# Triangular inverse by columns instead of rows, key decay as a per-token scalar, and smaller first query scalings in a hybrid decoder layer

## The chip, the core and the metric

The program runs on one core of a Trainium2 chip. The metric is the device time of one execution in microseconds (us). Before the change it is 2710.9 us, the median of three runs (2706.43 to 2711.62).

A core has a matrix engine (PE; its weight loads are listed apart as PEld), a vector engine (DVE), a scalar engine with activation functions (ACT), a general engine (POOL), and a queue that only issues DMAs (SP). Each works through its own list of instructions in order, and waits at an instruction until what it needs has been signalled.

## The reference

One layer, 2048 tokens of width 1024, all in fp32. One input projection feeds four heads of a gated delta rule and four heads of HGRN2; their outputs go through one output projection, a squared-ReLU MLP with 4096 hidden units, and a gated embedding. The change lies in the two token mixers:

```python
def gated_delta_rule_chunked(q, k, v, g, beta):
    ...
    gc = jnp.cumsum(g, axis=-1)
    decay = jnp.exp(jnp.where(causal, gc[..., :, None] - gc[..., None, :], -jnp.inf))
    k_beta = k * beta[..., None]
    v_beta = v * beta[..., None]
    lmat = jnp.einsum('bhncd,bhnsd->bhncs', k_beta, k) * decay
    a_mat = jnp.eye(c) + jnp.where(strict, lmat, 0.0)
    u = solve(v_beta)                          # a_mat^-1 v_beta
    w = solve(k_beta * jnp.exp(gc)[..., None]) # a_mat^-1 (k_beta exp(gc))
    ...
    def step(s, inp):
        v_new = u_n - w_n @ s
        o = qg_n @ s + qk_n @ v_new
        s = s * cd_n + kt_n^T @ v_new

def hgrn2_chunked(q, k, v, log_f):
    pair = jnp.exp(b_i - b_j)                  # causal
    att_ij = sum_d q_id k_jd pair_ijd
    o = att @ v + (q * exp(b)) @ s
    s = s * exp(b_last) + (k * exp(b_last - b))^T @ v
```

q and k of the delta rule are L2-normed over the head's 128 channels.

## The kernel before

The program has three stretches: an embedding projection at the start, the mixing stretch (about 40 to 1160 us), and the output projection, MLP and gate (from 1160 us on). Every large product is done as three products of fp32r halves, `128x512` matmuls.

**The mixing stretch** takes the tokens in four blocks of 512 (`q` 0 to 3) and in each the heads `h` 0 to 3. For each pair it runs eight projections of 24 matmuls each (line 1125), in three parts of eight; the end of a part is a tick. Beside these, one delta head (`gdn_mixer`) and one HGRN head (`hgrn_mixer`) are worked through. They are Python generators: each `yield` ends a step, and a table by hand (`A_STEPS`, `B_STEPS`; `A_LAST`, `B_LAST` for the last head) says at which tick, or half tick, a step is issued. So the order on **PE** and on **SP** is the order of the text, by these tables. The order on **DVE, ACT and POOL** is made by a planner that has its own costs for each instruction and may move an instruction ahead of others when it deems its inputs ready.

**A delta head** takes the 512 tokens in four chunks (`NC`) of 128. Its steps:

1. The decays: `gf` (the running sum of log decays, spread over all partitions by a DMA), `gc` (the same with tokens on the partitions), `e` (the decay matrix), `cd`, `tail`; `gf` becomes its exponential (lines 620 to 645).
2. Keys are turned, their norms taken; `cc` = beta/|k|^2, `ncc` = -cc, `inv` = |k| (lines 647 to 669).
3. Products of keys with keys and queries; `u` is the triangle's strict part with its sign, `qk` the weights of the output. Keys and queries are then multiplied with the decay `gf` (lines 688 to 690); the odd chunks' keys stand in another order (`odd`, `odd_back`). Values are turned into `vt`.
4. The four 32x32 diagonal blocks of each of the four triangles go through DRAM (`ud`) into `sys`, one system on eight partitions (`GR`), where each partition works on four (`GC`) of the 32 columns. Lines 715 to 726 are the **substitution** on DVE, two unknowns at a time: a product `pr` with the two columns of `sys` (line 720), a sum (line 723), and a correction of the second unknown by the first (line 725). Its result `xs` goes to DRAM (`xd`, line 730) and back into `xt` (line 737), which POOL has set to zero (line 735); DVE turns it into `xn` (line 739).
5. Two levels on PE, with copies on ACT, join the 32x32 inverses to `xt_full` (lines 755 to 781).
6. The **state chain**, chunk by chunk: `psa` = keys times state (line 786), `r` = vt*inv - psa on DVE (line 788), `psb` = inverse times r (line 791), `w` = cc*psb on ACT (line 793), `pss` (line 796) and the new state `S` on DVE (line 798), then the outputs `pso`. In `A_STEPS` the three products of a chunk stand 1.5, 1 and 1.5 ticks apart. The chain of one head runs while the next head's substitution is under way.

**An HGRN head** first scales queries and keys (lines 841 to 846), then runs six levels over doubling block sizes, where `side(t, n, s, late)` picks the late or early half of each pair of blocks.

Of the kernel before, what the change touches and what calls it, by code (L numbers as in the profile page):

```python
# [10 lines left out]
F32 = mybir.dt.float32  # L11
# [3 lines left out]
AF = mybir.ActivationFunctionType  # L15
ALU = mybir.AluOpType
AX = mybir.AxisListType
# [3 lines left out]
P = 128  # L21
# [3 lines left out]
QT = 512  # L25
NQ = T // QT
NC = QT // P
# [4 lines left out]
SB = 32  # L32
NB = P // SB
GR = P // (NC * NB)
GC = SB // GR
# [61 lines left out]
def trunk(ctx, tc, x, xT, pT, vecs, w_in, w_ab, gdn_a_log, gdn_dt_bias, w_out, w_up, w_down,  # L97
          w_ple, w_gate, consts, out):
    nc = tc.nc
    V, S, G, PE = nc.vector, nc.scalar, nc.gpsimd, nc.tensor  # L100
# [6 lines left out]
    sm = ctx.enter_context(tc.tile_pool(name="sm", bufs=3))  # L107
# [9 lines left out]
    def blk(c):  # L117
        return slice(c * P, (c + 1) * P)
# [8 lines left out]
    unit = cst[:, C_UNIT, :].rearrange("p (g i) -> p g i", i=SB)  # L127
# [258 lines left out]
    with ExitStack() as ectx:  # L386
        es = ectx.enter_context(tc.tile_pool(name="es", bufs=1))
        with tc.manual_schedule(engines={mybir.EngineType.SP, mybir.EngineType.Activation, mybir.EngineType.DVE}):
# [4 lines left out]
            xs = es.tile([P, NC, D], F32, name="xs")  # L393
# [63 lines left out]
    with mixers as mctx:  # L457
# [163 lines left out]
        def rows_of(g):  # L621
            return slice(g * SB, (g + 1) * SB)

        def gdn_mixer(q, h, live):

            n = f"g{q}_{h}"
# [10 lines left out]
            S.activation(cd, glast, AF.Exp)  # L637
            V.tensor_tensor(tail, glast, gc, ALU.subtract)
            S.activation(tail, tail, AF.Exp)
            e = mt(f"e_{n}", "e")  # L640
            V.tensor_tensor(by_pair(e), by_pair(gf), negm[:, None].broadcast_to([P, NC // 2, 2, P]), ALU.add)
            for c in range(NC):
# [4 lines left out]
            kT = live.pop("k")  # L647
            ssk = sm.tile([P, NC], F32, tag="ssk", name=f"ssk_{n}")
            rk = sm.tile([P, NC], F32, tag="rk", name=f"rk_{n}")
            both_cc = sm.tile([P, 2, NC], F32, tag="cc", name=f"cc_{n}")  # L650
            cc, ncc = both_cc[:, 0], both_cc[:, 1]
            inv = sm.tile([P, NC], F32, tag="inv", name=f"inv_{n}")
            psk = turned(kT, f"k{n}", pp)
            ktail = mt(f"kt_{n}", "ktail", 2)
# [7 lines left out]
            V.tensor_copy(rk, ssk)  # L662
            rsqrt(rk)
            yield
            V.tensor_tensor(cc, rk, rk, ALU.mult)
            V.tensor_tensor(cc, cc, beta, ALU.mult)
            V.tensor_scalar(ncc, cc, -1.0, None, ALU.mult)
            V.tensor_tensor(inv, ssk, rk, ALU.mult)
            yield

# [5 lines left out]
            for c in range(0, NC, 2):  # L676
# [8 lines left out]
                                           ps[:, a, 0, :].rearrange("p (b i) -> p b i", i=SB),  # L685
                                           ncc[:, c + a : c + a + 1], mine[:, ::-1] if a else mine, ALU.mult, ALU.mult)
                V.tensor_tensor(qk[:, c : c + 2, :], ps[:, :, 1, :], e[:, c : c + 2, :], ALU.mult)
            V.tensor_tensor(even(kT), even(kT), even(flat(gf)), ALU.mult)
            V.tensor_tensor(odd(kT), odd(kT), odd_back(flat(gf)), ALU.mult)
            V.tensor_tensor(qT, qT, flat(gf), ALU.mult)  # L690
            kg, qg = kT, qT
            yield
            psv = turned(live.pop("v"), f"v{n}", pp)
            vt = mt(f"vt_{n}", "vt", 2)
            S.activation(flat(vt), psv, AF.Copy)

            ud = dr.tile([NC, NB, SB, SB], F32, name=f"ud_{n}")
            for b in range(NB):
# [7 lines left out]
            for a in range(2):  # L706
# [2 lines left out]
            nc.sync.dma_start(  # L709
                flat(sys), ud.rearrange("c b j i -> (c b) (j i)")[:, None, :].broadcast_to([NC * NB, GR, SB * SB]))  # L710
            yield
            pr = mt(f"pr_{n}", "pr", 1, (P, 2 * GC, SB)).rearrange("p (two g) i -> p two g i", two=2)
            xs = mt(f"xs_{n}", "xs", 1, (P, GC, SB))

            V.tensor_copy(pr.rearrange("p two g (m e) -> p two g m e", e=2)[:, :, :, :, 0],
                          unit.rearrange("p g (m two) -> p two g m", two=2))
            V.tensor_copy(xs[:, :, 0:2], unit[:, :, 0:2])
            for i in range(0, SB, 2):
                if i:
                    V.tensor_tensor(pr[:, :, :, 0:i], xs[:, None, :, 0:i].broadcast_to([P, 2, GC, i]),  # L720
                                    sys[:, 0:i, i : i + 2].rearrange("p j two -> p two j")[:, :, None, :]
                                    .broadcast_to([P, 2, GC, i]), ALU.mult)
                    V.tensor_reduce(xs[:, :, i : i + 2].rearrange("p g two -> p two g"), pr[:, :, :, 0 : i + 1],
                                    AX.X, ALU.add)
                V.scalar_tensor_tensor(xs[:, :, i + 1], xs[:, :, i], sys[:, i, i + 1 : i + 2], xs[:, :, i + 1],
                                       ALU.mult, ALU.add)
                if i % 4 == 2:
                    yield
            xd = dr.tile([NC, NB, SB, SB], F32, name=f"xd_{n}")
# [2 lines left out]

            xt = mt(f"xt_{n}", "xt", 1, (P, NC, P // 2))
            xn = mt(f"xn_{n}", "xn", 1, (P, NC, P // 2))
            G.memset(xt, 0.0)
            for g in range(NB):
                nc.sync.dma_start(xt[rows_of(g), :, rows_of(g % 2)], xd[:, g].rearrange("c j i -> j c i"))
            yield
            V.transpose(flat(xn), flat(xt))
            yield  # L740

            def pairs(out, lhsT, rhs):
# [40 lines left out]
            for c in range(NC):  # L783
                s = state[h]
                psa = bank(f"psa_{n}_{c}", pp)[:, :P]
                PE.matmul(psa, kg[:, blk(c)], s, start=True, stop=True)
                r = m2.tile([P, P], F32, tag="r", name=f"r_{n}_{c}", bufs=1)
                V.scalar_tensor_tensor(r, vt[:, c, :], inv[:, c : c + 1], psa, ALU.mult, ALU.subtract)
                yield
                psb = bank(f"psb_{n}_{c}", pp)[:, :P]  # L790
                PE.matmul(psb, xt_full[:, c, :], r, start=True, stop=True)
                w = m2.tile([P, P], F32, tag="w", name=f"w_{n}_{c}")
                S.activation(w, psb, AF.Copy, scale=cc[:, c : c + 1])
                yield
                pss = bank(f"psc_{n}_{c}", pp)[:, :P]
                PE.matmul(pss, ktail[:, c, :], w, start=True, stop=True)
                s2 = mp.tile([P, P], F32, tag=f"S{h}", name=f"S_{n}_{c}", bufs=2)
                V.scalar_tensor_tensor(s2, s, cd[:, c : c + 1], pss, ALU.mult, ALU.add)
                PE.matmul(pso[:, blk(c)], s, qg[:, blk(c)], start=True, stop=False)
                PE.matmul(pso[:, blk(c)], w, qk[:, c, :], start=False, stop=True)  # L800
                state[h] = s2
                yield
            yield from finish(q, h, pso, live.pop("z"), q2, EPS * EPS * P, n)

        def side(t, n, s, late):

            h = n // 2
            return bass.AP(t.tensor, t.offset + (s if late else 0),
                           [list(t.ap[0]), [h - s if late else h + s, 2], [2 * s, h // (2 * s)], [1, s]])
# [13 lines left out]
        def hgrn_mixer(q, h, live):  # L823
# [14 lines left out]
            def by_half(t, s):  # L838
                return t.rearrange("p (a n s) -> p a n s", a=2, s=s)
# [2 lines left out]
            V.tensor_tensor(by_half(own, 1), side(qq, QT, 1, False), side(k, QT, 1, False), ALU.mult)  # L842
            V.tensor_tensor(side(k, QT, 1, False), side(k, QT, 1, False), side(f, QT, 1, True), ALU.mult)
            V.tensor_tensor(g, fv[:, :, 0], fv[:, :, 1], ALU.mult)
            V.tensor_tensor(qq, qq, f, ALU.mult)
            V.tensor_tensor(side(qq, QT, 1, True), side(qq, QT, 1, True), side(f, QT, 1, False), ALU.mult)
            yield
            S.activation(by_half(both[:, 1], 2), side(qq, QT, 2, True), AF.Copy)
            yield
# [1071 lines left out]
```

## Time and profile before

| | |
|---|---|
| median of three runs | 2710.9 us (2706.43, 2710.9, 2711.62) |
| the profiled execution's own time | 2706.48 us |
| its span, first to last instruction | 2704.7 us |
| granted PE clock over the span | 0.998 of full |

Busy times are unions over the instructions of an engine. A matmul's end is modelled and matmuls overlap, so a PE that is always busy can still be issuing late; where a weight load (PEld) waits, nothing is issued to PE. A row of a waits view names the waiting engine, tile and line, and behind the arrow whose signal came last; then the total in us, the number of waits, and the longest. In a view of groups a row holds the line, engine, operation, tiles, shape (out<-in) and count, then total busy us and the mean ns of one, then the engine's idle time just before.

### The profile page before, as it was taken

The page shows a single profiled execution, that of the slowest core. Times are in us where ns is not written, and L with a number is a line of the kernel's source. Part 1 is how long each engine was busy: PE and PEld are TensorE (multiplying, and loading weights), DVE is VectorE, ACT ScalarE, POOL GpSimd, SP SyncE. Part 2 cuts the span into 40 slices and gives each one's busy share as a digit, 9 for nine tenths or more (in the row PEclk, how much of TensorE's full clock was granted, in tenths as well). Part 3 has the DMA queues.
Part 4 walks back from the last instruction along what each step waited for, and adds up shares of the span by engine and source line. Part 5 has one row for each costly group of instructions (what it writes and reads, how often), then busy time and mean ns, then how long its engine had stood idle before and what let it go on. Part 6 is the DMA issues. An engine that isn't in the chain of part 4 may idle for free.

```text
span 2704.7 us, 38442 instructions
## 1 busy us (share of the span) xinstructions
PE 2654.4 (98%) x12745; PEld 2209.5 (82%) x12745; DVE 2030.6 (75%) x4208; ACT 1457.8 (54%) x2943; POOL 137.4 (5%) x147
## 2 busy tenths in 40 slices
PE   8999999999999999999999999999999999999999
PEld 6788888888888887878888878888888888888887
DVE  7778878787778777568888867767877765468775
ACT  7665555465446445566665555554554555565431
POOL 0000000000000000020000000001000001101000
PEclk9999999999999999999999999999999999999999
DMA  8777777667665666584666566667544465677663
GB/s 279 274 238 246 238 251 254 214 221 254 203 217 207 217 205 193 175 232 158 199 200 224 175 218 219 213 196 241 191 156 149 161 228 183 202 247 248 218 214 125
DMA packets 267766, 573.51 MB, mean 212 GB/s; under 512 B 55578, under 2 KB 60152, under 8 KB 250416
## 3 DMA queue, kind: packets, MB, share of 16 engines
q1 hardware_dynamic: 265264, 566.86, 63.2%
q0 software_dynamic: 2304, 4.20, 0.9%
q8 instruction: 101, 1.65, 0.3%
q14 instruction: 97, 0.79, 0.1%
HBM read 410.57 MB, written 160.37 MB: 211 GB/s over the span
## 4 chain that ended last, share of the span: by engine, by line
PE 53%; DMA 4%; DVE 2%; issue 1%; ACT 1%; POOL 1%; SPq 0%; POOLq 0%; DVEq 0%; ACTq 0%
PE u L1157 22%; PE d L1157 20%; PE mmg L1157 6%; PE mmo L1157 3%; DMA dr<-in_w_down_dram 1%; PE mme L199 1%; POOL acc_y L242 1%; DMA raw_out<-in_w_out_dram 1%; DMA rsb_g<-rd_g 0%; PE mmo L1008 0%; DMA rd_g<-m_g 0%; ACT sq_y L241 0%; DMA yo<-in_xT_dram 0%; DMA mixT<-mixd 0%; ACT da L172 0%
## 5 line engine op out<-in xcount | busy, mean ns | idle before, releaser
L1125 PE MATMUL mm<-xt,w 128*128 128x512 f32 x3072 | 784.2, 400 | 1.6 <-ACT zt_zg L599 1.3
L1125 PEld LDWEIGHTS mm<-xt,w 128*128 128x128 f32 x3072 | 553.3, 189 | 102.5 <-ACT zt_zg L599 1.8
L1157 PE MATMUL d<-db,da 128*128 128x512 f32 x2688 | 614.9, 389 | 2.2 <-ACT db L225 1.3
L1157 PEld LDWEIGHTS d<-db,da 128*128 128x128 f32 x2688 | 504.3, 188 | 109.2 <-ACT db L225 2.7
L1157 PE MATMUL u<-t,wu 128*128 128x512 f32 x2604 | 591.3, 389 | 0.0
L1157 PEld LDWEIGHTS u<-t,wu 128*128 128x128 f32 x2604 | 488.8, 188 | 101.4
L226 DVE TENSOR_TENSOR db<-db 128x512 fp32r<-128x512 f32 x224 | 161.6, 722 | 46.0 <-ACT db L225 45.5
L1544 DVE TENSOR_TENSOR u<-u,u 128x512 f32<-128x512 f32 x224 | 150.3, 682 | 54.4 <-PE u L1157 52.9
L1157 PE MATMUL mmg<-h2T,wg 128*128 128x512 f32 (+1 forms) x792 | 174.8, 383 | 0.0
L1157 PEld LDWEIGHTS mmg<-h2T,wg 128*128 128x128 f32 x792 | 145.6, 188 | 29.1
L225 ACT ACTIVATE db<-db 128x512 fp32r<-128x512 f32 x224 | 140.9, 629 | 49.4 <-DMA db<-hid 45.1
L1587 ACT ACTIVATE u<-u 128x512 f32<-128x512 f32 x128 | 80.7, 631 | 159.0 <-DVE u L1544 158.7
L173 DVE TENSOR_TENSOR da<-da 128x512 fp32r<-128x512 f32 x128 | 93.4, 729 | 81.2 <-ACT da L172 80.6
L1157 PE MATMUL mmo<-mixT,w_out 128*128 128x512 f32 x600 | 140.4, 395 | 4.1 <-DVE w_out L173 2.1
L172 ACT ACTIVATE da<-da 128x512 fp32r<-128x512 f32 x128 | 80.5, 629 | 116.0 <-DMA da<-sumd 97.9
L1157 PEld LDWEIGHTS mmo<-mixT,w_out 128*128 128x128 f32 x600 | 114.2, 191 | 29.0 <-DVE w_out L173 2.6
L173 DVE TENSOR_TENSOR da<-dr,da 128x512 fp32r<-128x512 f32 x96 | 68.9, 718 | 42.9 <-ACT da L172 41.0
L172 ACT ACTIVATE wu<-a 128x512 fp32r<-128x512 f32 x124 | 75.1, 623 | 45.7 <-DMA a<-in_w_up_dram 44.1
L720 DVE TENSOR_TENSOR pr_g<-xs_g,sys_g 128x16 f32<-128x16 f32 (+14 forms) x240 | 94.2, 392 | 5.6
L173 DVE TENSOR_TENSOR wu<-a,wu 128x512 fp32r<-128x512 f32 x124 | 85.7, 693 | 12.0 <-ACT wu L172 11.9
L1588 ACT ACTIVATE u<-u 128x512 f32<-128x512 f32 x128 | 80.4, 628 | 3.1
L172 ACT ACTIVATE da<-dr 128x512 fp32r<-128x512 f32 x96 | 60.5, 631 | 35.7 <-DMA dr<-in_w_down_dram 30.3
(390 smaller groups left out, 3821.4 us busy)
## 6 DMA issues: line engine op xcount, KB each, us to landing
w<-cache_in SPq DMA_DIRECT2D x96, 1024.0 KB
db<-hid SPq DMA_DIRECT2D x224, 256.0 KB
cache_in<-w SPq DMA_DIRECT2D x32, 1024.0 KB
hid<-u SPq DMA_DIRECT2D x128, 256.0 KB
da<-sumd SPq DMA_DIRECT2D x128, 256.0 KB
a<-in_w_up_dram SPq DMA_DIRECT2D x124, 256.0 KB
hid<-ht SPq DMA_DIRECT2D x96, 256.0 KB
dr<-in_w_down_dram SPq DMA_DIRECT2D x96, 256.0 KB
```

The costliest lines, as they stand in the source:

```text
L172: S.activation(t[:, 0], raw, AF.Copy)
L173: eng.tensor_tensor(t[:, 1], raw, t[:, 0], ALU.subtract)
L199: PE.matmul(ps, a, b, start=i == 0, stop=i == n - 1)
L225: S.activation(t[:, 0], plain(t), AF.Copy)
L226: V.tensor_tensor(t[:, 1], plain(t), t[:, 0], ALU.subtract)
L242: eng.tensor_tensor(acc, acc, sq, ALU.add)
L720: V.tensor_tensor(pr[:, :, :, 0:i], xs[:, None, :, 0:i].broadcast_to([P, 2, GC, i]), sys[:, 0:i, i : i + 2].rearrange("p j two -> p two j" ...
L1125: PE.matmul(ps, *terms[i], start=i == 0, stop=i == nt - 1)
L1157: PE.matmul(ps, a, b, start=start, stop=stop)
L1544: V.tensor_tensor(c[new], c[old], ps, ALU.add)
L1587: S.activation(c[k], c[k], AF.Relu)
L1588: S.activation(c[k], c[k], AF.Square)
```

## The change

- **Substitution.** It solves for the inverse's other triangle order: from the last two unknowns down to the first two. `sys` is now read along its rows (`sys[:, j:j+2, j+2:]`), where before two columns were read (`sys[:, 0:i, i:i+2]`). The correction inside each pair, before one instruction for each of the 16 pairs (line 725), is made for all pairs at once ahead of the loop: the upper row of each pair of `sys` is corrected by the lower one (two multiplications into `fix`, two additions), and so are the right hand sides in `base`.
- The result is `xn` as it comes back from DRAM, and DVE turns it into `xt` (before: `xt` came back, `xn` was made by the turn). POOL sets `xn` to zero.
- **Keys' decay.** Keys are no longer multiplied with `gf`; instead `r` = psa*eg - (v*inv), with `eg` = exp(gc) a scalar for each token. Its sign is turned, so `w` uses `ncc`, and `cc` is not kept. `inv` goes into `vt` by four scaled copies on ACT, one a chunk, in place of one copy.
- **HGRN.** The first scaling of queries, all 512 by `f` and then the late half by the early `f`, becomes the early half by its `f` and the late half by `g`, the product of the two.

```diff
+            both_cc = sm.tile([P, 2, NC], F32, tag="cc", name=f"cc_{n}")
+            eg, ncc = both_cc[:, 0], both_cc[:, 1]
+            S.activation(eg, gc, AF.Exp)
...
-            V.tensor_tensor(cc, rk, rk, ALU.mult)
-            V.tensor_tensor(cc, cc, beta, ALU.mult)
-            V.tensor_scalar(ncc, cc, -1.0, None, ALU.mult)
+            V.tensor_tensor(ncc, rk, rk, ALU.mult)
+            V.tensor_tensor(ncc, ncc, beta, ALU.mult)
+            V.tensor_scalar(ncc, ncc, -1.0, None, ALU.mult)
...
-            V.tensor_tensor(even(kT), even(kT), even(flat(gf)), ALU.mult)
-            V.tensor_tensor(odd(kT), odd(kT), odd_back(flat(gf)), ALU.mult)
...
-            S.activation(flat(vt), psv, AF.Copy)
+            for c in range(NC):
+                S.activation(vt[:, c, :], psv[:, blk(c)], AF.Copy, scale=inv[:, c : c + 1])
...
-            pr = mt(f"pr_{n}", "pr", 1, (P, 2 * GC, SB)).rearrange("p (two g) i -> p two g i", two=2)
+            pr = mt(f"pr_{n}", "pr", 1, (P, 2 * GC, SB)).rearrange("p (g two) i -> p g two i", two=2)
             xs = mt(f"xs_{n}", "xs", 1, (P, GC, SB))
-
-            V.tensor_copy(pr.rearrange("p two g (m e) -> p two g m e", e=2)[:, :, :, :, 0],
-                          unit.rearrange("p g (m two) -> p two g m", two=2))
-            V.tensor_copy(xs[:, :, 0:2], unit[:, :, 0:2])
+            fix = mt(f"fix_{n}", "fix", 1, (P, SB // 4, SB))
+            above, below = (sys.rearrange("p (m two) i -> p two m i", two=2)[:, r] for r in range(2))
+            next_to = bass.AP(sys.tensor, sys.offset + 1, [list(sys.ap[0]), [2 * SB + 2, SB // 2], [1, 1]])
+            mine, other = (unit.rearrange("p g (m two) -> p two g m", two=2)[:, r] for r in range(2))
+            base = pr.rearrange("p g two (m e) -> p two e g m", e=2)
+
+            V.tensor_copy(base[:, 1, 1], other)
+            V.tensor_tensor(base[:, 0, 1], other, next_to.rearrange("p m o -> p o m").broadcast_to([P, GC, SB // 2]),
+                            ALU.mult)
+            V.tensor_tensor(base[:, 0, 1], base[:, 0, 1], mine, ALU.add)
+            V.tensor_copy(xs[:, :, SB - 2 : SB], pr[:, :, :, SB - 1])
+            for part_m, part_i in ((slice(SB // 4, SB // 2), slice(SB // 2, SB)), (slice(0, SB // 4), slice(0, SB))):
+                width = part_i.stop - part_i.start
+                t = fix[:, :, :width]
+                V.tensor_tensor(t, below[:, part_m, part_i], next_to[:, part_m].broadcast_to([P, SB // 4, width]), ALU.mult)
+                V.tensor_tensor(above[:, part_m, part_i], above[:, part_m, part_i], t, ALU.add)
             for i in range(0, SB, 2):
+                j = SB - 2 - i
                 if i:
-                    V.tensor_tensor(pr[:, :, :, 0:i], xs[:, None, :, 0:i].broadcast_to([P, 2, GC, i]),
-                                    sys[:, 0:i, i : i + 2].rearrange("p j two -> p two j")[:, :, None, :]
-                                    .broadcast_to([P, 2, GC, i]), ALU.mult)
-                    V.tensor_reduce(xs[:, :, i : i + 2].rearrange("p g two -> p two g"), pr[:, :, :, 0 : i + 1],
-                                    AX.X, ALU.add)
-                V.scalar_tensor_tensor(xs[:, :, i + 1], xs[:, :, i], sys[:, i, i + 1 : i + 2], xs[:, :, i + 1],
-                                       ALU.mult, ALU.add)
+                    V.tensor_tensor(pr[:, :, :, j + 2 :], xs[:, :, None, j + 2 :].broadcast_to([P, GC, 2, i]),
+                                    sys[:, None, j : j + 2, j + 2 :].broadcast_to([P, GC, 2, i]), ALU.mult)
+                    V.tensor_reduce(xs[:, :, j : j + 2], pr[:, :, :, j + 1 :], AX.X, ALU.add)
...
-            G.memset(xt, 0.0)
+            G.memset(xn, 0.0)
             for g in range(NB):
-                nc.sync.dma_start(xt[rows_of(g), :, rows_of(g % 2)], xd[:, g].rearrange("c j i -> j c i"))
-            yield
-            V.transpose(flat(xn), flat(xt))
+                nc.sync.dma_start(xn[rows_of(g), :, rows_of(g % 2)], xd[:, g].rearrange("c j i -> j c i"))
+            yield
+            V.transpose(flat(xt), flat(xn))
...
-                PE.matmul(psa, kg[:, blk(c)], s, start=True, stop=True)
+                PE.matmul(psa, kT[:, blk(c)], s, start=True, stop=True)
-                V.scalar_tensor_tensor(r, vt[:, c, :], inv[:, c : c + 1], psa, ALU.mult, ALU.subtract)
+                V.scalar_tensor_tensor(r, psa, eg[:, c : c + 1], vt[:, c, :], ALU.mult, ALU.subtract)
-                S.activation(w, psb, AF.Copy, scale=cc[:, c : c + 1])
+                S.activation(w, psb, AF.Copy, scale=ncc[:, c : c + 1])
...
-            V.tensor_tensor(qq, qq, f, ALU.mult)
-            V.tensor_tensor(side(qq, QT, 1, True), side(qq, QT, 1, True), side(f, QT, 1, False), ALU.mult)
+            V.tensor_tensor(side(qq, QT, 1, False), side(qq, QT, 1, False), side(f, QT, 1, False), ALU.mult)
+            V.tensor_tensor(side(qq, QT, 1, True), side(qq, QT, 1, True), by_half(g, 1), ALU.mult)
```

More of the change, by code (lines that the diff above doesn't have):

```diff
@@ L649, in gdn_mixer @@
             rk = sm.tile([P, NC], F32, tag="rk", name=f"rk_{n}")
-            both_cc = sm.tile([P, 2, NC], F32, tag="cc", name=f"cc_{n}")
-            cc, ncc = both_cc[:, 0], both_cc[:, 1]
             inv = sm.tile([P, NC], F32, tag="inv", name=f"inv_{n}")
@@ L687, in gdn_mixer @@
                 V.tensor_tensor(qk[:, c : c + 2, :], ps[:, :, 1, :], e[:, c : c + 2, :], ALU.mult)
-            V.tensor_tensor(even(kT), even(kT), even(flat(gf)), ALU.mult)
-            V.tensor_tensor(odd(kT), odd(kT), odd_back(flat(gf)), ALU.mult)
             V.tensor_tensor(qT, qT, flat(gf), ALU.mult)
-            kg, qg = kT, qT
+            qg = qT
             yield
```

## The prediction

> **What bounds the kernel now.** I read the page's busy times first, then busy times by stretch, then who waits for whom in the mixing stretch, first for PE's weight loads, then for its matmuls.
>
> ```profile
> PE 2654.4 (98%) x12745; PEld 2209.5 (82%) x12745; DVE 2030.6 (75%) x4208; ACT 1457.8 (54%) x2943; POOL 137.4 (5%) x147
> ```
>
> ```profile
> 40.00:1040.00 1000.00, 977.83 (x5306) 828.65 (x5307) 779.48 (x2212) 552.78 (x1417) 58.65 (x78) 1.00 0.70 232
> 1040.00:1160.00 120.00, 114.58 (x592) 95.72 (x591) 77.56 (x180) 64.34 (x127) 4.13 (x4) 1.00 0.57 180
> ```
>
> The columns of the second view are the stretch, its length, and the busy time of PE, PEld, DVE, ACT and POOL, then the granted clock. The change touches nothing outside 40 to 1160 us, and removes no matmul inside it. So it can only win what PE loses there by waiting: 1000 - 977.8 and 120 - 114.6, 27.6 us of visible idle time. DVE is busy 779.5 + 77.6 = 857.0 us of these 1120, or 77%: not the bound, but full enough for queues to form. The waits say whether PE stands behind them. Weight loads:
>
> ```profile
> PEld psb_g L791 <- DVE r_g L788: 12.2, 16, 1.9
> PEld psa_g L786 <- DVE S_g L798: 8.7, 13, 1.7
> PEld psc_g L796 <- ACT w_g L793: 4.7, 8, 1.3
> PEld kk_g L681 <- ACT y_qg L573: 3.7, 4, 1.6
> PEld psp_g L744 <- DVE xn_g L739: 3.5, 3, 1.9
> PEld nrm_g L280 <- DVE hl_g L173: 2.9, 4, 1.2
> ...
> PEld at_h L875 <- ACT keys_h L880: 2.3, 2, 2.1
> ```
>
> Matmuls:
>
> ```profile
> PE psb_g L791 <- DVE r_g L788: 7.0, 8, 1.5
> PE psa_g L786 <- DVE S_g L798: 3.2, 5, 1.3
> ...
> PE psp_g L744 <- DVE xn_g L739: 2.2, 3, 1.4
> ...
> PE psp_g L744 <- DVE xn_g L764: 1.6, 2, 0.8
> ```
>
> The loss lies between the two views: a weight load normally runs under the matmul ahead of it, so its idle time says too much; a matmul's end is modelled late, so PE's says too little. The state chain (psb, psa) and the first join (psp) lose 12.2 + 8.7 + 3.5 = 24.4 by the first and 7.0 + 3.2 + 2.2 + 1.6 = 14.0 by the second; I take the middle, 19.2 us, as what waits for DVE at the places that the change is near. The timeline shows what such a wait is made of:
>
> ```profile
> 938.88 0.43 DVE L843 TENSOR_TENSOR qk_h<-qk_h,f_h 128x256 f32<-128x256 f32 x1
> 939.22 0.68 DVE L607 TENSOR_TENSOR og_h<-pso_h,zt_gh 128x512 f32<-128x512 f32 x1
> 939.82 0.68 DVE L173 TENSOR_TENSOR hl_h<-osq_h,hl_h 128x512 fp32r<-128x512 f32 x1
> 940.42 0.68 DVE L845 TENSOR_TENSOR qk_h<-qk_h,f_h 128x512 f32<-128x512 f32 x1
> 941.02 0.34 DVE L788 SCALAR_TENSOR_TENSOR r_g<-vt_g,inv_g,psa_g 128x128 f32<-128x128 f32 x1
> ...
> 941.41 0.30 PEld L791 LDWEIGHTS psb_g<-r_g,xt_full 128*128 128x128 f32 x2 [1.19 <-DVE r_g L788]
> ```
>
> DVE works without a pause, `r` stands behind a queue, and PE waits 1.19 us. It is a queue's lag and not a slow `r`: whatever shortens the work ahead shortens it.
>
> **The change part by part, on DVE.** The groups by shape (busy us, mean ns, idle before):
>
> ```profile
> L725 DVE SCALAR_TENSOR_TENSOR xs_g<-xs_g,sys_g 128x4 f32<-128x4 f32 x256 | 57.6, 225 | 22.7 <-DMA sys_g<-ud_g 17.3
> L720 DVE TENSOR_TENSOR pr_g<-xs_g,sys_g 128x16 f32<-128x16 f32 (+14 forms) x240 | 94.2, 392 | 5.6
> L720 DVE TENSOR_TENSOR pr_g<-xs_g,sys_g 128x240 f32<-128x240 f32 x16 | 9.6, 601 | 0.3
> L720 DVE TENSOR_TENSOR pr_g<-xs_g,sys_g 128x16 f32<-128x16 f32 x16 | 2.8, 176 | 0.4
> L842 DVE TENSOR_TENSOR att_h<-qk_h 128x256 f32<-128x256 f32 x16 | 6.7, 418 | 0.2 <-PE t_ih L594 0.2
> L888 DVE TENSOR_TENSOR gg_h<-gg_h 128x128 f32<-128x128 f32 x16 | 4.7, 293 | 0.5
> L888 DVE TENSOR_TENSOR gg_h<-gg_h 128x64 f32<-128x64 f32 x16 | 3.6, 223 | 0.4
> L888 DVE TENSOR_TENSOR gg_h<-gg_h 128x16 f32<-128x16 f32 x16 | 2.8, 174 | 0.5
> L715 DVE COPY pr_g<-cst 128x128 f32<-128x128 f32 x16 | 4.5, 282 | 0.0
> L717 DVE COPY xs_g<-cst 128x8 f32<-128x8 f32 x16 | 3.7, 230 | 14.3 <-DMA xd_g<-xs_g 14.2
> L845 DVE TENSOR_TENSOR qk_h<-qk_h,f_h 128x512 f32<-128x512 f32 x16 | 10.9, 683 | 0.0
> L688 DVE TENSOR_TENSOR y_kg<-y_kg,gf_g 128x256 f32<-128x256 f32 x16 | 6.7, 416 | 0.0
> ```
>
> For one head, of 16:
> - The 16 pair corrections go: 57.6 / 16 = 3.60 us.
> - The old start goes: 0.282 + 0.230 = 0.51. The new one is a copy and two products or sums of 64 elements, at the 64-element row's 223 each, and a small copy at 0.23: 0.90 more.
> - `fix`: a product and a sum of 8x16 = 128 elements (293 each) and of 8x32 = 256 (418 each): 1.42 more.
> - The key multiplications of lines 688 and 689 go: 2 x 0.416 = 0.83. `r` stays one instruction of the same shape.
> - HGRN's line 845 has 256 elements for 512: 683 - 418 = 0.27 less. Line 846 keeps its size.
> - Line 720. At 16 elements it costs what another product does (176 against 174), at 240 far more (601, where 256 cost 418). It reads `sys` down columns, 32 elements apart; now it reads along rows. No row shows that form. From above its price is today's, 94.2 / 16 = 5.89 us. From below it is the line through 174 at 16 and 418 at 256 elements (1.02 ns an element, 158 ns fixed): 15 x 0.158 + 1920 x 0.00102 = 4.32. I take the lower, since the form is nearest to those rows, whose operands are likewise in several short pieces: 1.57 less. The sums of line 723 keep their sizes.
>
> Net: 3.60 + 0.51 + 0.83 + 0.27 + 1.57 - 0.90 - 1.42 = 4.46 us less, times 16 heads 71 us, or 8.3% of 857.0. With line 720 as dear as today it is 2.89 a head, 46 us.
>
> Two waits move. Line 717 may be issued by the planner right behind the previous head's solution, and then holds DVE until that has landed in DRAM: 14.2 us of DVE standing idle, everything behind it with it. In the new text the first write into `xs` comes after a product that reads `sys`; it can't be hoisted so far, and that wait goes. The wait for `sys` (17.3 us) stays, with nine instructions of 2.3 us behind it where there were one or two small ones; `r` and `S` of the previous head can stand behind them. That is the loss side (below).
>
> **On ACT, POOL, SP and PE.**
>
> ```profile
> L659 ACT ACTIVATE kt_g<-t_kg,tail_g 128x128 f32<-128x128 f32 x64 | 18.0, 369 | 0.0
> L637 ACT ACTIVATE cd_g<-gf_g 128x4 f32<-128x4 f32 x16 | 3.3, 209 | 10.9 <-DMA gf_g<-gd 10.7
> L695 ACT ACTIVATE vt_g<-t_vg 128x512 f32<-128x512 f32 x16 | 9.6, 598 | 2.9 <-PE t_vg L594 2.5
> ```
>
> Four scaled copies cost as the keys' four do, 18.0 / 16 = 1.13 for 0.60; `eg` is one more small exponential of 0.21. That is 0.73 us a head, 12 us in all on an engine that is half idle. Behind it stand w, the queries' silu and HGRN's keys, for which the weight loads wait 4.7 + 3.7 + 2.3 = 10.7 us. ACT gets 12 / 617 = 2% fuller; I charge a tenth of the 10.7, 1 us. In return w (4.7) follows `r`, and gains with it; I let the two cancel.
>
> ```profile
> SPq L730 <- DVE xs_g L725: 27.4, 6, 6.9
> ```
>
> ```profile
> POOL xt_g L735 <- PE psd_g L744: 52.3, 9, 13.9
> ```
>
> SP waits for the substitution's end, with weight reloads queued behind; a shorter one frees it earlier. No DMA is added. POOL's zeroing waits for the previous head's last join; with `xn` it waits for a product one step earlier. POOL is 5% busy, so I cost it at nothing; if it came late, the loads into `xn` would be late next, then psp. The turn on DVE leaves the path of the first psp (the weight loads' 3.5 us), since psp reads `xn` as it lands, and is due a step later. On PE, psa reads the plain keys, ready earlier; no cost.
>
> **The sum.** Of the 19.2 us I take 60%. A wait behind `r` or `S` is 12.2 / 16 = 0.76 or 8.7 / 13 = 0.67 us long. In the later two thirds of a substitution DVE's queue is lighter by 1 to 4 us, more than such a wait, so it goes; in the first third it is heavier by 2.32 - 0.51 = 1.8 us less the first corrections, and it stays or grows. 0.6 x 19.2 = 11.5, and some 0.5 for SP and the vanished wait of line 717: 12 us. The profiled execution would take 2706.5 - 12 = 2694.5. It is the lowest but one of the four times known (2706.43 to 2711.62, median 2710.9); off the median it is **2699 us**.
>
> Its own range: all waits of the psb, psa, psc and psp rows, 29.1 us, plus SP's side gone is 2682 at the best; a third of 14.0 gone is 2706. With line 720 unchanged (46 / 71 of the gain) it is 2703.
>
> **The rivals.**
>
> *No change, 2711 (2706 to 2716).* PE is busy 98%, and DVE's work is beside it. For it: `r` has 1.5 ticks of cover, and where `psa` came late DVE was idle, so a lighter DVE changes nothing there. Against it: the timeline above, and 24.4 us of waits that name DVE. The planner also lays out DVE's list anew, and new collisions may replace the old ones. The Trainium skill (Perfetto Trace Analysis, Identifying the Most-Contended Engine) says to optimize the engine with the highest occupancy, and to judge PE by its weight loads; by that rule, with PEld at 82% and DVE at 75%, work taken off DVE would give nothing. The trace agrees on the order of the engines, but its waits show PE standing behind DVE.
>
> *Slower, 2722.* The nine instructions at the substitution's start come as one block once `sys` has landed, and the planner puts them ahead of `r` or `S` of the previous head. It decides if the block is due within 1.5 ticks of one of these, for most of 15 heads. Price: 1.8 us more in front, about 1 us of it beyond the cover, 15 x 1 = 15, with what the end wins (some 4) spent: 2711 + 11. For it: DVE has already waited 17.3 us there. Against it: three small instructions of the old loop fall out of the same stretch, and the steps of the first third are few.
>
> **How the numbers follow.** Forecast 0.65, no change 0.20, slower 0.15. Two executions differ by up to 0.2%, 5 us, which is what can be told from no change. Faster than 2705.5 is nearly all of the first case, 0.64; within 0.2% 0.21; slower 0.15. The range is 2686 to 2714: the best end of the first case has little weight, and the upper end takes in the second.
>
> **What would show it.** Right: DVE busy in 40 to 1160 us lower by 46 to 71 us, no line of pair corrections, line 720's successor at 240 elements near 400 ns, no wait of `xs` for `xd`; psb's and psa's waits on DVE together below 10 us in the weight loads' view; PE's visible idle time there below 20. Wrong: DVE lighter as worked out, with those waits as long as before or moved to the start of the substitution or to kk, at_h and psc on ACT; or the new line 720 as dear as the old.

## The result, and the profile after

| | before | after |
|---|---|---|
| median | 2707.85 us (2706.43 to 2711.62, 5 runs) | 2682.55 us (2680.95 to 2686.9, 5 runs) |
| ratio | | 0.9905, 95% interval 0.989 to 0.9919 |
| profiled execution, own time and span | 2706.48, 2704.7 us | 2686.9, 2685.1 us |

The kernel is 25 us faster, where 12 were forecast. The profiled execution of after is the slowest of its five, so its span shows 19.6 of the 25; what is read from traces in this section compares these two profiled executions.

The MLP's first product, behind the mixing stretch, starts 21.8 us earlier, at 1252.6 us for 1274.4 (first before, then after; the times are of the first and the last start):

```profile
L1157 PE MATMUL u<-t,w_u x84: 389/389/389, 1274.4 to 1293.7; 128*128 128x512 f32 x84
L1166 PE MATMUL u<-t,w_u x84: 389/389/389, 1252.6 to 1271.8; 128*128 128x512 f32 x84
```

Busy times from the page of after, and in the mixing stretch (columns as before: PE, PEld, DVE, ACT, POOL, clock):

```profile
PE 2646.8 (99%) x12745; PEld 2213.1 (82%) x12745; DVE 1966.1 (73%) x4016; ACT 1493.1 (56%) x3025; POOL 136.5 (5%) x147
```

```profile
40.00:1040.00 1000.00, 988.17 (x5392) 845.79 (x5391) 728.72 (x2065) 593.99 (x1511) 58.36 (x78) 1.00 0.71 236
1040.00:1140.00 100.00, 98.81 (x515) 83.78 (x514) 66.58 (x140) 60.74 (x119) 4.64 (x5) 1.00 0.58 190
```

DVE is 64.5 us lighter over the whole program (2030.6 to 1966.1). PE's idle time in the stretch is 11.8 + 1.2 = 13 us, where 27.6 stood. ACT is 35.3 us busier (1457.8 to 1493.1), where the prediction charged 12. What it left out is in this row of after:

```profile
L642 ACT ACT_TABLE_LOAD x13 | 16.7, 1283 | 0.2
```

Line 642 is the new exponential `eg`. An `ACT_TABLE_LOAD` is an instruction of its own, listed ahead of some activations; the trace of before has 68 of them, that of after 86. The 18 more at 1.283 us are 23.1 us, and with the 12 that were charged they make the 35.

Who PE waits for in the mixing stretch, the weight loads of after first, then its matmuls:

```profile
PEld mm L1134 <- issue: 4.6, 2, 3.5
PEld psa_g L795 <- DVE S_g L807: 2.6, 4, 1.2
PEld nrm_g L280 <- DVE hl_g L173: 2.3, 3, 1.5
PEld psc_g L805 <- ACT w_g L802: 2.1, 5, 0.9
PEld mm L1134 <- ACT e_g L646: 2.0, 2, 1.1
PEld psb_g L800 <- DVE r_g L797: 1.8, 3, 1.0
PEld kk_g L682 <- ACT y_qg L573: 1.7, 2, 1.1
```

```profile
PE mm L1134 <- DVE acc_vg L564: 3.1, 1, 3.1
...
PE psa_g L795 <- DVE S_g L807: 1.0, 2, 0.8
...
PE psb_g L800 <- DVE r_g L797: 0.6, 1, 0.6
```

psb waited 12.2 us for `r`, now 1.8; psa 8.7 for `S`, now 2.6; psc 4.7, now 2.1; psp's 3.5 for the turn is gone, though one of 1.5 us, put down to POOL, is new. The first row's 3.5 us stand at 77 us, where in before two waits of 1.8 and 1.6 us stand (for `zt_zg` and `y_vg`), so little of it is new. The groups of DVE in after, and below them the row of `r` before:

```profile
L733 DVE TENSOR_TENSOR pr_g<-xs_g,sys_g 128x16 f32<-128x16 f32 (+14 forms) x240 | 69.4, 289 | 5.1
L733 DVE TENSOR_TENSOR pr_g<-xs_g,sys_g 128x240 f32<-128x240 f32 x16 | 6.5, 405 | 0.2
L729 DVE TENSOR_TENSOR sys_g<-sys_g,fix_g 128x128 f32<-128x128 f32 (+1 forms) x32 | 11.3, 354 | 0.0
L728 DVE TENSOR_TENSOR fix_g<-sys_g 128x128 f32<-128x128 f32 (+1 forms) x32 | 11.3, 353 | 0.0
L721 DVE TENSOR_TENSOR pr_g<-cst,sys_g 128x64 f32<-128x64 f32 x16 | 4.5, 278 | 15.7 <-DMA sys_g<-ud_g 15.4
L797 DVE SCALAR_TENSOR_TENSOR r_g<-psa_g,cc_g,vt_g 128x128 f32<-128x128 f32 x64 | 22.2, 346 | 60.1 <-PE psa_g L795 60.1
```

```profile
L788 DVE SCALAR_TENSOR_TENSOR r_g<-vt_g,inv_g,psa_g 128x128 f32<-128x128 f32 x64 | 21.9, 343 | 35.8 <-PE psa_g L786 35.8
```

The products cost 69.4 us for 94.2. Ahead of `r`, DVE sits idle 60.1 us until psa is done, where it was 35.8: it has caught up, and now waits for PE more often. A place in the timeline like the one in the prediction, where three of the same instructions meet ahead of `r` in another block of tokens:

```profile
476.81 0.68 DVE L607 TENSOR_TENSOR og_h<-pso_h,zt_gh 128x512 f32<-128x512 f32 x1
477.42 0.68 DVE L173 TENSOR_TENSOR hl_h<-osq_h,hl_h 128x512 fp32r<-128x512 f32 x1
478.01 0.42 DVE L854 TENSOR_TENSOR qk_h<-qk_h,f_h 128x256 f32<-128x256 f32 x1
478.35 0.35 DVE L797 SCALAR_TENSOR_TENSOR r_g<-psa_g,cc_g,vt_g 128x128 f32<-128x128 f32 x1
...
480.69 0.42 PEld L800 LDWEIGHTS psb_g<-r_g,xt_full 128*128 128x128 f32 x2
```

Here `r` ends at 478.35 + 0.35 = 478.70, two microseconds before psb's weight load, and psb has no wait.

### The profile page after: what moved, and what is told of

The parts are those of the page before. It is cut to its first block, busy times and chain, and to the rows that moved or that the text cites. A ratio compares the mean times of both kernels' runs of the same rounds, so it can differ in the third digit from the quotient of the medians.

```text
span 2685.1 us, 38292 instructions
## 1 busy us (share of the span) xinstructions
PE 2646.8 (99%) x12745; PEld 2213.1 (82%) x12745; DVE 1966.1 (73%) x4016; ACT 1493.1 (56%) x3025; POOL 136.5 (5%) x147
## 4 chain that ended last, share of the span: by engine, by line
PE 65%; DMA 4%; issue 3%; ACT 2%; DVE 1%; POOL 1%; SPq 0%; POOLq 0%; ACTq 0%; DVEq 0%
PE u L1166 22%; PE d L1166 18%; PE mm L1134 9%; PE mmg L1166 6%; PE mmo L1166 4%; PE mme L199 1%; POOL acc_y L242 1%; DMA dr<-in_w_down_dram 1%; DMA ud_g<-u_g 1%; DMA da<-sumd 0%; PE at_h L884 0%; DMA gf_g<-gd 0%; DMA raw_out<-in_w_out_dram 0%; PE mmo L1017 0%; DMA sys_g<-ud_g 0%
## 5 line engine op out<-in xcount | busy, mean ns | idle before, releaser
L242 POOL TENSOR_TENSOR acc_y<-acc_y,sq_y 128x512 f32<-128x512 f32 x28 | 38.4, 1372 | 764.3 <-ACT sq_y L241 764.3
```

The costliest lines, as they stand in the source:

```text
L242: eng.tensor_tensor(acc, acc, sq, ALU.add)
```

## The experiments

Each kernel is compared with the kernel before on its own chip; ratios are to that, with 95% intervals, and one per mil is 2.7 us. The kernel after, run again on the chip of `col_read`, `old_turn` and `sub_hgrn`, gave the same ratio:

> The kernel after itself, on the same chip as these, as the mark for them: 0.9905 of before, within 0.989 to 0.992.

0.9906 (0.989 to 0.9923).

**One part alone.** The first three start from the kernel before. `sub_only` takes over lines 712 to 750 of after (the substitution, and `xn` and `xt` exchanged):

> The kernel before with the new substitution and its swapped xn and xt alone; keys and HGRN as before. By the theory that the gain is DVE's queue getting shorter (Q), this part takes 3.6 + 0.5 + 1.6 - 0.9 - 1.4 = 3.4 of the 4.5 us a head off DVE, so about three quarters of the 25 us: 2685 to 2692, with psb's and psa's waits on DVE down from 12.2 and 8.7 us to under 6 each. By the theory that the keys' decay gives most (psa's operand is ready earlier) it stays above 2700. By the theory that the planner's new order happened to be a good one, the parts don't add up to the whole.

0.9891 (0.9871 to 0.9912): the whole gain, where three quarters were expected. psb waits 1.8 us and psa 2.6, as in after. `keys_only` takes over `eg`, `ncc`, the scaled `vt` and the plain keys:

> The kernel before with the keys' decay as a scalar alone. Q: 0.83 us a head less on DVE of 4.46, so 3 to 6 us: 2702 to 2705. By the theory that the plain keys matter, over 12 us: under 2696. With ACT's extra 0.7 us a head counting for more than I charged: 2708 or more.

1.001 (0.9999 to 1.0022): no gain, though DVE's busy time fell by 9.9 us. ACT's rose by 33.9, with the same 18 more table loads as in after. So the part takes work off DVE and puts more on ACT; whether the two cancel, or neither counts, was not tested. `hgrn_only`:

```diff
-            V.tensor_tensor(qq, qq, f, ALU.mult)
-            V.tensor_tensor(side(qq, QT, 1, True), side(qq, QT, 1, True), side(f, QT, 1, False), ALU.mult)
+            V.tensor_tensor(side(qq, QT, 1, False), side(qq, QT, 1, False), side(f, QT, 1, False), ALU.mult)
+            V.tensor_tensor(side(qq, QT, 1, True), side(qq, QT, 1, True), by_half(g, 1), ALU.mult)
```

> The kernel before with HGRN's first query scalings in halves alone. Q: 0.27 us a head of 4.46, 1 to 2 us: 2706. A new planner order by luck could give anything within 5 us of 2708.

0.9994 (0.998 to 1.0008): nothing that can be told from none.

**The hoisted wait.** `xs_two`:

```diff
-            xs = mt(f"xs_{n}", "xs", 1, (P, GC, SB))
+            xs = mt(f"xs_{n}", "xs", 2, (P, GC, SB))
```

> The kernel before with two buffers for xs, so that the early first write of xs need not wait until the last solution has landed in DRAM (14.2 us of DVE idle in the view of before). By the theory that this hoisted wait, standing in front of r and S, made a large part of PE's waits (H): 8 to 15 us faster, 2693 to 2700. Q: the wait is part of the queue, but DVE has 23% slack beside it: 2 to 5 us, 2703 to 2706.

0.9994 (0.9983 to 1.0005). But it missed what it was to test. In its view of waits DVE still stands idle at that write:

```profile
DVE xs_g L717 <- DMA xd_g<-xs_g: 10.9, 9, 2.2
```

With a second buffer the planner issued the write a whole head earlier, and it waited there. `late_xs` makes it depend on `sys`:

```diff
-            V.tensor_copy(xs[:, :, 0:2], unit[:, :, 0:2])
+            V.scalar_tensor_tensor(xs[:, :, 0:2], sys[:, 0:GC, 0:2], 0.0, unit[:, :, 0:2], ALU.mult, ALU.add)
```

> The kernel before, whose first write into xs now also reads sys (times zero), so that the planner can't issue it ahead of sys. Two buffers for xs did not take that wait away: the write was issued a head earlier still and waited again (10.9 us of 14.2). By H (that wait, standing in front of r and S, makes a large part of PE's waits): 6 to 15 us faster than before. By the theory that the length of the substitution counts (L): within 3 us of before.

0.9986 (0.9976 to 0.9996), 4 us. The wait is gone, but psb's and psa's are nearly as before (12.5 and 7.4): it stood elsewhere for the most part.

**The substitution taken apart.** `fwd_fix` goes forward and down the columns as before, with the old turn, but corrects the pairs at once:

```diff
+            first, second = (sys.rearrange("p j (m two) -> p two j m", two=2)[:, r] for r in range(2))
...
+            for part_m, part_j in ((slice(0, SB // 2), slice(0, SB // 2)), (slice(SB // 4, SB // 2), slice(SB // 2, SB))):
+                width = part_m.stop - part_m.start
+                t = fix[:, :, :width]
+                V.tensor_tensor(t, first[:, part_j, part_m], next_to[:, :, part_m].broadcast_to([P, SB // 2, width]),
+                                ALU.mult)
+                V.tensor_tensor(second[:, part_j, part_m], second[:, part_j, part_m], t, ALU.add)
...
-                V.scalar_tensor_tensor(xs[:, :, i + 1], xs[:, :, i], sys[:, i, i + 1 : i + 2], xs[:, :, i + 1],
-                                       ALU.mult, ALU.add)
```

> The kernel before with the pairs corrected at once, but forward and down the columns of sys as before, and with xt loaded and xn turned as before. DVE: 3.6 + 0.5 - 0.9 less, minus the corrections at column price, about 2 us: 1 to 1.5 us a head off, half or less of the new substitution's 3.4. L: 8 to 14 us faster, and no wait of xs for xd either. By the theory that the swapped turn (psp reads the loaded tile) gives most: at most 4 us faster.

0.9955 (0.9942 to 0.9967): 12 us, of which late_xs's 4 are probably a part, since here too `xs` is first written after `sys`. Its weight loads:

```profile
PEld psb_g L801 <- DVE r_g L798: 11.7, 12, 2.0
PEld psa_g L796 <- DVE S_g L808: 7.6, 10, 1.5
```

The state chain's own waits have hardly changed; what fell are others (psp's, the norms', kk's). `col_read` is the kernel after with the products reading down columns, so that it computes no inverse:

```diff
-                                    sys[:, None, j : j + 2, j + 2 :].broadcast_to([P, GC, 2, i]), ALU.mult)
+                                    sys[:, j + 2 :, j : j + 2].rearrange("p k two -> p two k")[:, None]
+                                    .broadcast_to([P, GC, 2, i]), ALU.mult)
```

> The kernel after, whose products read sys down columns again (the wrong ones, so what is computed is no longer the inverse), all else as in the kernel after: the products cost 94 us again where they cost 69. By the theory that the reading along rows is what freed the state chain (R): psb's and psa's waits on DVE back above 12 us, 10 to 17 us slower than after. By the theory that the swapped turn did it (T): within 4 us of after, psb below 5.

0.9944 (0.9929 to 0.9959), 3.8 per mil or 10 us slower than after. The products' group, and the first three waits of the weight loads:

```profile
L733 DVE TENSOR_TENSOR pr_g<-xs_g,sys_g 128x16 f32<-128x16 f32 (+14 forms) x240 | 93.9, 391 | 5.1
```

```profile
PEld psb_g L801 <- DVE r_g L798: 8.6, 12, 1.6
PEld psa_g L796 <- DVE S_g L808: 4.7, 7, 1.2
PEld psc_g L806 <- ACT w_g L803: 4.4, 6, 1.3
```

The products cost their old 94 us, and half of the state chain's waits come back: psb's and psa's are 13.3 us, where they were 20.9 before and 4.4 after. `old_turn` is the kernel after with `xt` loaded and `xn` turned as before, so that the wrong triangle is joined:

> The kernel after with the old way back: the loaded tile is xt and DVE turns it into xn, which the first psp needs (so the joined inverse is of the wrong triangle; the work is the same). T: 6 to 15 us slower than after, psp's wait on xn back to 3 us and more, and psb behind it. R: 1 to 4 us slower, the 3.5 us of psp's wait at most.

0.9913 (0.9898 to 0.9928): 2 us slower than after at the middle, within its uncertainty; only one wait of psp on the turn, 1.4 us, comes back. The three parts add up: 4.5 per mil (fwd_fix), 3.8 (col_read against after), 0.7 (old_turn) make 9.0 of 9.5. Each is uncertain by one to two per mil, so that they meet so closely is partly luck.

**Idle work in three places.** `pad_pairs`, on the kernel after:

```diff
                     V.tensor_reduce(xs[:, :, j : j + 2], pr[:, :, :, j + 1 :], AX.X, ALU.add)
+                V.scalar_tensor_tensor(fix[:, 0, :GC], xs[:, :, j], sys[:, j, j + 1 : j + 2], xs[:, :, j + 1], ALU.mult, ALU.add)
```

> The kernel after with 16 idle corrections a head back in the loop of the substitution, at the places of the old ones, their results not used: 3.6 us a head of DVE more there, all else as in the kernel after. L and the theory of DVE's queue in general: most of the gain goes, 2698 to 2706 where after is near 2681; psb's and psa's waits on DVE back to 15 us or more. By H or the swapped turn: up to 5 us slower than after.

0.9936 (0.9917 to 0.9955): 8 us slower than after, less than half of what was expected; psa waits 6.1 us, psb only 1.9. `pad_else` has 16 instructions of the same shape in one piece behind the scaling of the queries:

```diff
             qg = qT
+            for i in range(SB // 2):
+                V.scalar_tensor_tensor(fix[:, 0, :GC], qT[:, :GC], inv[:, 0:1], qT[:, GC : 2 * GC], ALU.mult, ALU.add)
```

> The kernel after with the same 16 idle instructions a head, but in one piece at the place where the key multiplications stood, ahead of the substitution. By the theory that DVE's whole load counts: as slow as the pad in the substitution. By L (what counts is DVE's work in the stretch where the substitution stands beside the state chain of the previous head): 0 to 8 us slower than after, the pad's 3.6 us being absorbed by slack or delaying u.

0.9908 (0.9886 to 0.9929), no slower than after. Busy time by stretch, first of pad_else, then of after:

```profile
40.00:1140.00 1100.00, 1090.44 (x5927) 934.29 (x5926) 847.46 (x2465) 656.17 (x1631) 67.81 (x89) 1.00 0.70 233
```

```profile
40.00:1140.00 1100.00, 1086.98 (x5905) 929.57 (x5904) 795.29 (x2204) 654.73 (x1630) 63.00 (x83) 1.00 0.70 232
```

DVE is busy 847 of 1100 us, 77%, just as in the kernel before, and the whole gain is kept. On the pages DVE's busy time is 2013.8 us for 1966.1, 47.7 more. So DVE's load as such was not the cause; where the work stands is.

**Known and unknown time.** col_read's DVE list is the kernel after's: all 4016 instructions of the trace stand in the same order, and only their durations differ. An idle instruction, though, is one that the planner sees and orders around. `pad_seven` has 7 of pad_pairs' instructions a head, `pad_chain` has 6 on which the next instruction waits:

```diff
+                if i % 4 == 2 and i < 24:
+                    V.scalar_tensor_tensor(xs[:, :, j], sys[:, j, 0:GC], 0.0, xs[:, :, j], ALU.mult, ALU.add)
```

> The kernel after with 7 idle corrections a head in the loop of the substitution, 7 x 0.225 x 16 = 25 us on DVE, as much as the column reads cost. By the theory that a given time on DVE in this stretch costs the same whatever it is (time): 8 to 12 us slower than after, as the column reads were. By the theory that the planner, who makes a new order around instructions it knows and had the same order for the column reads, absorbs most of it (plan): 1 to 5 us slower, psb's and psa's waits together below 8 us.

0.9909 (0.9895 to 0.9922), 1 us slower than after. The timeline of pad_seven shows that this pad was lighter than meant:

```profile
594.75 0.24 DVE L735 TENSOR_REDUCE xs_g<-pr_g 128x8 f32<-128x88 f32 x1
595.03 0.23 DVE L737 SCALAR_TENSOR_TENSOR fix_g<-xs_g,sys_g 128x4 f32<-128x4 f32 x1
595.17 0.25 DVE L733 TENSOR_TENSOR pr_g<-xs_g,sys_g 128x96 f32<-128x96 f32 x1
```

The product behind the idle instruction starts 0.14 us after it, before its 0.23 are over, since it needs nothing from it: 7 x 0.14 x 16 = 16 us, and pad_pairs' was 36, not 58. DVE's busy time on the pages grew by less still: from 1966.1 us in after to 1977.3 in pad_seven (11.2 more) and 1993.8 in pad_pairs (27.7 more), beside 1989.4 in col_read (23.3 more). Hence pad_chain:

> The kernel after with 6 instructions a head in the chain of the substitution that leave xs as it is (adding zero times sys), 25 us of DVE in all, as the column reads cost. By the theory that a given time in DVE's list in this stretch costs the same, known to the planner or not (time): 8 to 12 us slower than after, 0.994 to 0.995 of before. By the theory that the planner makes room for what it knows (plan): 0 to 4 us slower, 0.9905 to 0.992.

0.9916 (0.9902 to 0.9929), 3 us slower than after. Its timeline:

```profile
594.12 0.17 DVE L737 SCALAR_TENSOR_TENSOR xs_g<-sys_g,xs_g 128x4 f32<-128x4 f32 x1
594.32 0.19 DVE L733 TENSOR_TENSOR pr_g<-xs_g,sys_g 128x32 f32<-128x32 f32 x1
```

0.20 us from start to start, so 6 x 0.20 x 16 = 19 us in the chain at most; DVE's busy time grew by 10.8 us (to 1976.9). At col_read's rate (10 us for 24.5 of products, 23.3 of busy time) 19 us would give a ratio of 0.9935, just outside the interval, and 10.8 us one of 0.9924, inside it. So the times do not show that known time costs less than unknown. The waits lean that way: psb's and psa's weight loads wait 1.8 + 3.2 = 5.0 us in pad_chain, 13.3 in col_read.

There is a rival that no run tests: the place in the loop. Of the 24.5 us that the column reads add, 18.9 fall on the eight products of 128 elements and more, the later half of the loop. pad_pairs has 8 of its 16 instructions there (8 x 0.14 x 16 = 18 us), pad_chain 2 of 6 (6.4 us) and pad_seven 3 of 7 (6.7 us). The measured costs, 10, 8, 3 and 1 us, follow these numbers too. The 8 us are those of pad_pairs, whose instructions the planner knew.

**Towards a faster one.** `sub_hgrn` leaves the keys' part out; `sub_again` repeats sub_only:

> The kernel before with the new substitution and HGRN's halves, without the keys' scalar decay. The keys' part alone was 0 to 2 per mil slower than before; if that holds beside the new substitution too (ACT's 0.7 us a head weigh more than DVE's 0.8), this is 2 to 5 us faster than after; if the parts don't mix so, equal to it.

> The kernel before with the new substitution and its turn alone, once more. If the keys' scalar decay costs what it cost alone (0 to 2 per mil), this beats the kernel after: 0.988 to 0.990. If the two are equal: 0.990 to 0.991.

0.9897 (0.988 to 0.9913) and 0.9896 (0.9877 to 0.9914). With sub_only's 0.9891 that is three times below after's 0.9905 and 0.9906, by 2 to 4 us; the intervals overlap, so by the times it is not shown that leaving the keys' part out is faster. The traces lean that way: the MLP's first product starts at 1243.0 us (sub_only), 1245.2 (sub_again) and 1248.3 (sub_hgrn), in after at 1252.6 and 1248.4. `fix_pool` moves the larger half of the corrections from DVE to POOL:

```diff
+                E = G if width == SB else V
-                V.tensor_tensor(t, below[:, part_m, part_i], next_to[:, part_m].broadcast_to([P, SB // 4, width]), ALU.mult)
-                V.tensor_tensor(above[:, part_m, part_i], above[:, part_m, part_i], t, ALU.add)
+                E.tensor_tensor(t, below[:, part_m, part_i], next_to[:, part_m].broadcast_to([P, SB // 4, width]), ALU.mult)
+                E.tensor_tensor(above[:, part_m, part_i], above[:, part_m, part_i], t, ALU.add)
```

> The kernel after with the larger half of the pair corrections (256 elements, a product and a sum) on POOL, which is 5% busy: 0.84 us a head less on DVE in the stretch that counts, and that half is needed only in the second half of the loop. If what is left of psb's and psa's waits (3 to 5 us) still hangs on DVE there: 1 to 4 us faster than after, 2677 to 2680. If POOL, which waits in order for its square roots, comes late: slower than after by up to 10 us, with waits of pr on POOL.

0.9929 (0.9916 to 0.9943), 6 us slower than after. The feared wait of DVE for POOL's corrections does not stand in its view. What came back are psa's and psb's waits:

```profile
PEld psa_g L796 <- DVE S_g L808: 5.4, 6, 1.9
...
PEld psb_g L801 <- DVE r_g L798: 3.8, 6, 1.3
```

The move did not lighten DVE. Its busy time is 1968.6 us, for 1966.1 in after, though 13.5 us of corrections left it. The timeline shows why:

```profile
656.21 0.63 POOL L729 TENSOR_TENSOR fix_g<-sys_g 128x256 f32<-128x256 f32 x1 [20.03 <-DVE xs_g L724]
656.33 0.55 DVE L734 TENSOR_TENSOR pr_g<-xs_g,sys_g 128x16 f32<-128x16 f32 x1
...
656.90 0.18 DVE L736 TENSOR_REDUCE xs_g<-pr_g 128x8 f32<-128x24 f32 x1
656.92 0.73 POOL L730 TENSOR_TENSOR sys_g<-sys_g,fix_g 128x256 f32<-128x256 f32 x1
657.12 0.57 DVE L734 TENSOR_TENSOR pr_g<-xs_g,sys_g 128x32 f32<-128x32 f32 x1
```

A DVE product that starts while POOL works on a correction ends only after it (656.88 and 656.84; 657.69 and 657.65). So it is with all 33 DVE instructions of two operands (`TENSOR_TENSOR`) that start beside one; the 21 sums, which read one operand, are not held up. The products of 16, 32 and 48 elements took 333, 367 and 409 ns on average, where they take 169, 191 and 208 in after. So the start of the substitution, a chain in which each step needs the one before, became slower. That this makes up all of the 6 us is not shown; the planner's order differs too.

## Why the prediction was wrong

Right, by its own steps:
- **The prices on DVE.** Line 720's successor was put at the lower bound, 4.32 us a head or 69.1 in all, and took 69.4; 405 ns at 240 elements, near the 400 named. The corrections were put at 1.42 us a head and took (11.3 + 11.3) / 16 = 1.41. DVE lost 64.5 us, within the 46 to 71 named. The hoisted write's wait is gone.
- **The place.** The gain came out of psb's, psa's and psp's waits. psb's and psa's fell to 4.4 us together, below the 10 named; `r` stood behind a queue.
- **The slower rival** did not come. The substitution starts with eight instructions (the prediction counts nine), but psb and psa do not wait behind them for long, as the next list shows.
- **The no-change rival** fell too. The Trainium skill (Perfetto Trace Analysis, Identifying the Most-Contended Engine) says to optimize the engine with the highest occupancy first. That work taken off another engine would give nothing is the prediction's reading; here it gave 25 us, with PE at 98% busy. pad_else shows what is true in it: whether DVE is busy 77% or 72% of the stretch changes nothing by itself. Where its work stands does.

**The step that failed is the sum**: "I take the middle, 19.2 us", and "Of the 19.2 us I take 60%". Both factors were too small, and two terms beside them were wrong.
- *60%.* It let the waits in the first third of a substitution stay or grow, since DVE's queue is heavier there. But the weight loads' waits of the same rows (psb, psa, psp) went from 24.4 to 4.4 us, 82% less, and the matmuls' from 14.0 to 1.6. Laid against the product of the substitution that ran last before it, only 4.6 of psb's and psa's 20.9 us of waits stood in the first third (products of up to 80 elements) in before, and these fell as well, to 1.1.
- *The middle of two views.* With psc, which follows `r`, the weight loads' waits went from 29.1 to 6.5 us, 22.6 less, where the matmuls' fell by 12.4 without it. The MLP's first product came 21.8 us earlier. In col_read the same holds: psb's and psa's weight loads wait 13.3 us for 4.4, 8.9 more, and the time is 10 more. Over all 18 traces, a straight line through the length of the stretch (from the first projection matmul to the MLP's first product) rises by 0.99 us for each us that the weight loads of these four products wait, and by 2.0 for each us ahead of their matmuls. Over all rows of the two views it is 0.85 and 1.6. (These slopes are fits, one execution for each run.) So the loss did lie between the views, as the prediction says, but near the weight loads' end: the matmuls' view held about half of it. Together the two factors forecast 11.5 us from these waits, and 22.6 went.
- *What was let cancel, or put small.* psc's 4.7 us, set off against ACT, fell by 2.6, and kk's 3.7 by 2.0. For the hoisted write and SP half a microsecond was charged; late_xs measured 4 (1 to 6) for the write. ACT was charged 12 us and took 35, as it loads tables 18 times more; the keys' part, which brings them, gave nothing.

**Not every microsecond of DVE counted.** The prediction spread 4.46 us a head evenly. The keys' 0.83 and HGRN's 0.27 gave nothing that can be told from none (keys_only, hgrn_only), and 16 instructions ahead of the substitution cost nothing (pad_else). The row reads' 1.57 a head were worth 10 us. That the substitution is what counts is shown: sub_only, sub_again and sub_hgrn have the whole gain, and its parts, taken apart, come near to it. Why time in it costs unequally is open. One reason would be the planner: it gave row and column reads the same order, so it seems to price them alike, and the column reads came later than planned. Another is the place in the loop, by which the later half counts most. No run changes the planner's prices, and none pads the later half alone. How far the planner's new orders differ by luck is open too.

## What to carry to other kernels

Where PE's order is fixed and other engines feed it, count the waits of its weight loads, not the idle time ahead of its matmuls, and look which of them a change can reach before scaling by an engine's busy share. Price a change by the place of the work and not by the engine's whole load: 48 us more of DVE's busy time ahead of the substitution cost nothing, 23 us in the substitution cost 10 us. The first thing to look for in a group is a form that costs more than its neighbours of the same size (601 ns at 240 elements beside 418 at 256). Where an activation moves among others, count the table loads too. Work moved to POOL can hold up the DVE products that run beside it. And a wait that names a buffer need not go with a second buffer: the planner may issue the writer earlier still.

## What the runs showed of the hardware

A DVE product of 240 fp32 elements took 600 ns when one operand was read 32 elements (128 bytes) apart (col_read; 601 in before) and 405 when it was read in rows (after). The slope over the sizes was 1.9 ns an element against 1.05, and at 16 elements there was hardly a difference (172 and 169). The Trainium skill (SBUF — State Buffer, Door 1: The DMA port swizzle) says that each access that crosses to a new 16-byte line pays a penalty. The traces agree as far as they go: in this form the time of an element nearly doubled.

Two DVE instructions with no dependence overlapped by about 0.09 us (0.14 from start to start where the first took 0.23). The times of small instructions, added up, therefore overstate what putting them in costs: pad_pairs' 256 add up to 56.8 us, and DVE's busy time grew by 27.7.

A DVE product with two operands was held up when it started while POOL worked on a product of its own: in fix_pool one of 16 elements took 0.55 us, where it takes 0.17 in after, and ended 0.04 us after POOL's. All 33 of the kind ended after POOL's, 31 of them within 0.1 us. A DVE sum over one operand, started in the same place, was not held up (0.18 us for 0.17).

A table load on ACT took 1.283 us each time (86 in after).
